# DRAM-to-DRAM additions of the halves of w_down: 128 rows outermost, in quarters of 32 rows

## The chip, the cores and the metric

The kernel runs on one core of a Trainium2 chip. The metric is the device time of one execution in microseconds (us). TensorE (PE) multiplies matrices, VectorE (DVE), ScalarE (ACT) and GpSimd (POOL) do elementwise work, SyncE (SP) only issues transfers. Transfers are issued from SP (and a few from ACT) on one kind of queue and from POOL on another, and all of them run on the core's 16 DMA engines.

## The reference

One layer of a bidirectional mixer is followed by a convolutional feed-forward network, over 1024 latent tokens and 128 prompt tokens of width 1024. The part that matters here is the feed-forward network (FFN_HIDDEN is 2816):

```python
def conv_ffn(h, w_up, conv_w, conv_b, w_down, grid):
    u = dw_conv(h @ w_up, conv_w, conv_b, grid)
    gate, up = jnp.split(u, 2, axis=-1)
    return (jax.nn.silu(gate) * up) @ w_down
```

The result is scaled, added to the residual and normalised. Everything is float32; the kernel splits each operand of a product into a high and a low part and multiplies three times (high by high, high by low, low by high).

## The kernel before

**Both products of the network use seven block products instead of eight** (the Strassen-Winograd scheme), so sums of blocks of the weights are needed. For `w_up` the sums are made in SBUF by POOL, for `w_down` they are made in DRAM, by transfers.

**The up stage** runs over 22 channel blocks, `for c in range(NHID + 1)`; block c is 128 gate and 128 up columns. For each block PE does the seven products `up(c, p)` (line 1322), two halves of the prompt's product (`up_prompt`, line 1526) and two transposes. ACT copies the prompt's result once a block (`late`, line 1615; one such instruction for each block, which makes it a good clock of the stage). DVE does the 3x3 convolution (line 1462) and the prompt's width-3 convolution (line 1479).

POOL works one block ahead: it makes the low parts of the weights (line 62, called from `split_slots`), the sums of `w_up` (`weight_sums`, lines 1313 to 1316), the product of gate and up (line 1558) and sums over tokens (lines 1416 to 1419, every second block). It issues, in its own order, the store of the block's result (`scr_g`, line 1559, 576 KB), the store of the token sums (`scr_s`, line 1420, 1 MB, every second block), and the transfers on `w_down` described below. One such instruction of POOL stands between its elementwise instructions, and what comes later on POOL waits until it is issued.

`load_row` (line 1293) loads the raw weights of a later block into the tile `ra` (and `sr`) from SP: four transfers of 256 KB for each block. `ra` holds one block, so a load is issued only when POOL has read the old contents, and POOL's next `weight_sums` (line 1313) waits until it has landed. PE then waits for the low parts (`wul`, line 62).

**The sums of w_down.** `w_down` is (2816, 1024). With p = 0..127, j = 0..10 and h = 0, 1, row (2j + h) * 128 + p is row p of pair j of half h. Four DRAM scratch tensors `scr_t[i]` of shape (11, 128, 512) are filled: `scr_t[0]` and `scr_t[2]` by copying one block and adding another, `scr_t[1]` and `scr_t[3]` by copying `scr_t[0]` and `scr_t[1]` and adding another block. A copy is one transfer of 2816 KB (line 1430). An addition is a transfer with `accum_op=ALU.add`, which reads its destination and its source and writes the destination; it is issued in four pieces of 3, 3, 3 and 2 values of j (line 1435). That makes 20 transfers, 4 copies and 16 additions, in a list `sums_todo`. `second_half` takes one from the list for each block from the second on, right after the product of gate and up:

```python
        last = nc.gpsimd.tensor_tensor(accg, accg, accu, op=ALU.mult)
        nc.gpsimd.dma_start(scr_g[c], accg)
        if sums_todo and c > 0:
            with tc.issue_after(last.ins):
                sums_todo.pop(0)()
```

So each block of the up stage has one of these transfers, followed in POOL's queue by the store of `scr_g`. The order in the list is: two copies, four pieces of `scr_t[0]`, four of `scr_t[2]`, a copy from `scr_t[0]` to `scr_t[1]`, four pieces, a copy from `scr_t[1]` to `scr_t[3]`, four pieces.

**The down stage** runs seven products of 11 pairs (`product`, line 1732) and the prompt's (line 1783). `load_pair` loads, for each pair j, one block of tokens (`scr_g`, `scr_s`) and one of weights (`w_down`, or `scr_t[i][j]` for the products 4 to 7), on SP's queue, in a fixed sequence that begins before the up stage is over. `load_gates` puts the load of `modrC` in the same queue, and `make_gates` (line 1663) needs it between the last pairs of the first product.

Of the kernel before, what the change touches and what calls it, by code (L numbers as in the profile page):

```python
# [13 lines left out]
ALU = mybir.AluOpType  # L14
# [3 lines left out]
P = 128  # L18
# [7 lines left out]
NPAIR = 11  # L26
# [20 lines left out]
def kernel(ctx: ExitStack, tc: tile.TileContext, ins, outs, stop=None):  # L47
    nc = tc.nc
# [40 lines left out]
    scr_t = [dram.tile([NPAIR, P, 512], F32, name=f"scr_t{i}") for i in range(4)]  # L89
# [72 lines left out]
    w_down = ins["w_ffn_down"][0]  # L162
# [37 lines left out]
    lo_t, hi_t, lo_f, hi_f = slice(0, 512), slice(512, NS), slice(0, 512), slice(512, D)  # L200
# [167 lines left out]
    for i in range(2):  # L368
        nc.vector.memset(modA[i], 0.0)
        t = modA[i][:, :]  # L370
# [1040 lines left out]
    def token_sums(j):  # L1411
# [10 lines left out]


    halves = [
        [w_down.rearrange("(j h p) f -> h j p f", h=2, p=P)[h][:, :, fs] for fs in (lo_f, hi_f)] for h in range(2)
    ]
    sums_todo = []

    def sum_copy(i, src):
        sums_todo.append(lambda: nc.gpsimd.dma_start(scr_t[i], src))  # L1430

    def sum_add(i, src):
        for j in range(0, NPAIR, 3):
            js = slice(j, min(j + 3, NPAIR))
            sums_todo.append(lambda js=js: nc.gpsimd.dma_start(scr_t[i][js], src[js], accum_op=ALU.add))

    sum_copy(0, halves[0][1])
    sum_copy(2, halves[1][1])
    sum_add(0, halves[0][0])
    sum_add(2, halves[0][1])  # L1440
    sum_copy(1, scr_t[0])
    sum_add(1, halves[1][1])
    sum_copy(3, scr_t[1])
    sum_add(3, halves[1][0])

    def conv_rows(u, ch, acc, ra=0, rb=NROW):
# [400 lines left out]
def build(nc, shapes, outs_kind="ExternalOutput", stop=None):  # L1847
    ins = {
        n: nc.dram_tensor(f"in_{n}_dram", s, dt, kind="ExternalInput").ap() for n, (s, dt) in shapes.items()
    }  # L1850
    outs = [
        nc.dram_tensor(f"out_{i}_dram", s, F32, kind="ExternalOutput").ap() for i, (s, _) in enumerate(_OUTS)
    ]
    with tile.TileContext(nc, schedule_with_timeline_sim=True) as tc:
        kernel(tc, ins, outs, stop)
# [14 lines left out]
```

## Time and profile before

| what | value |
|---|---|
| median of 3 runs | 1804.22 us (1801.51 to 1809.65) |
| the profiled execution, its own time | 1807.15 us |
| its span from first to last instruction | 1805.4 us |
| PE busy | 1635.6 us, 91% of the span |
| DVE, ACT, POOL busy | 1189.3, 754.0, 738.9 us |
| mean granted TensorE clock | 0.947 |

In the page's second part the span is cut into 40 slices of 45 us. The up stage fills slices 21 to 34, the down stage the rest. The line PEclk is the clock that TensorE was granted, in tenths of full speed; a matmul takes longer where it is lower. Times "to landing" run from the issue of a transfer to the last of its bytes. In the chain of waits, "DMA" is time in which the next instruction waited for a transfer.

### The profile page before, as it was taken

The page shows a single profiled execution, that of the slowest core. Times are in us where ns is not written, and L with a number is a line of the kernel's source. Part 1 is how long each engine was busy: PE and PEld are TensorE (multiplying, and loading weights), DVE is VectorE, ACT ScalarE, POOL GpSimd, SP SyncE. Part 2 cuts the span into 40 slices and gives each one's busy share as a digit, 9 for nine tenths or more (in the row PEclk, how much of TensorE's full clock was granted, in tenths as well). Part 3 has the DMA queues.
Part 4 walks back from the last instruction along what each step waited for, and adds up shares of the span by engine and source line. Part 5 has one row for each costly group of instructions (what it writes and reads, how often), then busy time and mean ns, then how long its engine had stood idle before and what let it go on. Part 6 is the DMA issues. An engine that isn't in the chain of part 4 may idle for free.

```text
span 1805.4 us, 24012 instructions
## 1 busy us (share of the span) xinstructions
PE 1635.6 (91%) x9050; PEld 1367.4 (76%) x9050; DVE 1189.3 (66%) x1720; ACT 754.0 (42%) x1397; POOL 738.9 (41%) x535
## 2 busy tenths in 40 slices
PE   7999989999999998898789978778787888799998
PEld 2788867998999998786568856656676677578886
DVE  4555453365766768546799967657676787758765
ACT  4433434434544354215554423323333343356544
POOL 2401111232423231112579958667775878400001
PEclk9999997999999999999899998888898899999999
DMA  9133350231413231638213533324433435678863
GB/s 361 53 117 112 105 166 36 78 97 44 129 39 108 66 128 49 251 137 298 93 46 133 162 99 94 99 67 105 145 95 91 137 114 157 200 261 323 304 192 123
DMA packets 191117, 244.37 MB, mean 135 GB/s; under 512 B 38900, under 2 KB 135394, under 8 KB 188954
## 3 DMA queue, kind: packets, MB, share of 16 engines
q1 hardware_dynamic: 142583, 168.54, 29.0%
q0 software_dynamic: 47808, 73.63, 13.1%
q8 instruction: 71, 1.16, 0.3%
q10 hardware_dynamic: 611, 0.68, 0.1%
q14 instruction: 44, 0.36, 0.1%
HBM read 186.95 MB, written 78.71 MB: 147 GB/s over the span
## 4 chain that ended last, share of the span: by engine, by line
PE 59%; DMA 17%; POOL 12%; DVE 6%; issue 4%; ACT 1%; SPq 1%; POOLq 0%; DVEq 0%; ACTq 0%
PE mm L580 15%; DMA ra<-in_w_ffn_up_dram 12%; PE mm L594 6%; POOL wul L62 5%; PE u L1322 5%; PE lv L862 5%; PE xb L1732 5%; PE yb L1732 5%; PE mm L720 3%; PE yb L1783 2%; PE u L1215 2%; DMA scr_g<-acc 2%; PE o L938 1%; PE x L903 1%; PE mm L485 1%
## 5 line engine op out<-in xcount | busy, mean ns | idle before, releaser
L1462 DVE SCALAR_TENSOR_TENSOR acc<-u,convc,acc 128x945 f32<-128x945 f32 (+2 forms) x352 | 426.8, 1218 | 12.1 <-ACT acc L1450 5.7
L62 POOL TENSOR_TENSOR wl<-raw,wh 128x1024 fp32r<-128x1024 f32 x42 | 102.5, 2444 | 272.5 <-ACT wh L123 255.2
L580 PE MATMUL mm<-h1h,wh 128*128 128x384 f32 x528 | 184.2, 349 | 0.1
L580 PE MATMUL mm<-h1l,wh 128*128 128x384 f32 x528 | 180.6, 342 | 0.0
L580 PE MATMUL mm<-h1h,wl 128*128 128x384 f32 x528 | 180.6, 342 | 0.0
L62 POOL TENSOR_TENSOR wul<-sr,wuh 128x512 fp32r<-128x512 f32 (+1 forms) x68 | 134.4, 1978 | 11.4 <-ACT wuh L1308 11.1
L862 PE MATMUL lv<-Q,m 64*128 64x128 f32 (+1 forms) x1008 | 126.2, 295 | 12.5 <-DVE Q L871 6.7
L879 DVE COPY_PREDICATED S<-masks,lv 128x384 f32<-128x384 uint8 x168 | 98.8, 588 | 57.6 <-PE lv L862 57.5
L62 POOL TENSOR_TENSOR wul<-ra,wuh 128x1024 fp32r<-128x1024 f32 x46 | 128.3, 2788 | 13.3 <-ACT wuh L123 7.2
L855 ACT ACTIVATE m<-k 128x384 f32<-128x384 f32 x126 | 69.8, 556 | 140.3 <-DVE k L873 118.1
L862 PEld LDWEIGHTS lv<-Q,m 64*128 64x128 f32 (+1 forms) x1008 | 107.3, 191 | 26.7 <-issue 11.0
L871 DVE TENSOR_TENSOR Q<-Q,fb 128x384 f32<-128x384 f32 x126 | 90.3, 717 | 56.0 <-PE lv L862 55.6
L1322 PE MATMUL u<-b22h,wul 128*128 128x512 f32 x88 | 47.3, 537 | 65.8 <-POOL wul L62 65.8
L580 PEld LDWEIGHTS mm<-h1h,wh 128*128 128x128 f32 x528 | 99.8, 189 | 5.5 <-issue 3.7
L1707 POOL TENSOR_TENSOR sq<-sq,mhalf 128x1 f32<-128x1 f32 x9 | 11.1, 1237 | 222.5 <-DVE sq L1704 222.5
L1479 DVE SCALAR_TENSOR_TENSOR acc<-x,convc,acc 128x127 f32<-128x127 f32 x88 | 30.3, 344 | 108.2 <-ACT acc L1475 108.2
L580 PEld LDWEIGHTS mm<-h1l,wh 128*128 128x128 f32 x528 | 99.8, 189 | 1.5 <-issue 0.8
L580 PEld LDWEIGHTS mm<-h1h,wl 128*128 128x128 f32 x528 | 99.7, 189 | 0.7 <-issue 0.6
L1308 ACT ACTIVATE wuh<-ra 128x1024 fp32r<-128x1024 f32 x44 | 46.3, 1051 | 100.6 <-DMA ra<-in_w_ffn_up_dram 87.4
L123 ACT ACTIVATE wh<-raw 128x1024 fp32r<-128x1024 f32 x55 | 58.1, 1058 | 67.6 <-DMA raw<-in_w_in_dram 23.3
L1313 POOL TENSOR_TENSOR sr<-ra 128x512 f32<-128x512 f32 x22 | 30.8, 1402 | 132.4 <-DMA ra<-in_w_ffn_up_dram 129.8
L594 PE MATMUL mm<-wh,h1h 128*128 128x256 f32 x288 | 83.2, 289 | 0.0
(344 smaller groups left out, 4747.8 us busy)
## 6 DMA issues: line engine op xcount, KB each, us to landing
ra<-in_w_ffn_up_dram SPq DMA_DIRECT2D x88, 256.0 KB, 10.3
raw<-in_w_in_dram SPq DMA_DIRECT2D x32, 512.0 KB, 4.4
raw<-in_w_ada_dram SPq DMA_DIRECT2D x32, 512.0 KB, 3.7
scr_g<-acc POOLq DMA_DIRECT2D x22, 576.0 KB, 24.9
scr_s<-late POOLq DMA_DIRECT2D x11, 1024.0 KB, 16.0
scr_t<-in_w_ffn_down_dram POOLq DMA_DIRECT2D x12, 768.0 KB, 27.3
wa<-in_w_ada_dram SPq DMA_DIRECT2D x16, 512.0 KB, 5.9
raw<-in_w_out_dram SPq DMA_DIRECT2D x13, 512.0 KB, 10.0
```

What stands on the lines that cost most here:

```text
L62: return eng.tensor_tensor(out, full, hi.bitcast(F32), op=ALU.subtract)
L123: nc.scalar.activation(hi, raw, AF.Copy)
L580: mm(ps, a[:, kt, :], h[kt][b], start=(n == 0), stop=(n == 23))
L594: mm(ps, h[kt][t // 3][:, ts_], a[:, kt % 4, :], start=(n == 0), stop=(n == 23))
L720: mm(ps, lhs, ws[f][wi][:, cs], start=(f + n == 0), stop=(f == 6 and n == 2))
L855: nc.scalar.activation(aps(kmix, 0, [[2 * h, NB], [h, 2], [1, h]]), aps(kf_, 0, [[2 * h, NB], [BL + h, 2], [1, h]]), AF.Copy)
L862: last = mm(ps[:, i, :], kmix[r0:r1, i * P : (i + 1) * P], aps(Qf_, i * P, dims, r0, r1), start=True, stop=True,)
L871: nc.vector.tensor_tensor(qm, qm, aps(ff_, 2 * h - 1, [[BL - h, 2], [2 * h, NB], [0, h]]), op=ALU.mult)
L879: nc.vector.copy_predicated(S_, masks[:, lev : lev + 1, :].to_broadcast([P, 3, P]), ps)
L1322: last = mm(dst, W[x][:, a, kt, :], HB[y][b][:, kt, :], start=(start and n == 0), stop=(stop and n == 11), skip_group_check=True,)
L1462: last = nc.vector.scalar_tensor_tensor(o, u3[:, r0 + dy : r1 + dy, c0 + dx : c1 + dx], wc(3 * (dy + 1) + dx + 1), o, op0=ALU.mult, op1=AL ...
L1732: anchor["down"] = mm(banks[i], w[a][:, ts_], w[b][:, 512:1024], start=(start and j == 0 and n == 0), stop=(j == NPAIR - 1 and n == 2), sk ...
```

## The change

The two sides of every copy and addition get another order of dimensions: row p outermost, then pair j. The sources become (128, 11, 512) views of `w_down`, and `sums` are (128, 11, 512) views of the same scratch tensors. An addition is again four pieces, but a piece is now 32 of the 128 rows of all 11 pairs (704 KB) instead of all 128 rows of 3 or 2 pairs (768 or 512 KB). The bytes of each scratch tensor, the list of 20 transfers and its order stay.

In the built program the number and order of instructions on PE, DVE, ACT and SP are the same as before, with the same number of transfers. On POOL the sizes of the 20 transfers differ, and in one of the 22 blocks the store of `scr_s` stands behind one elementwise instruction instead of ahead of it. Before, a copy's destination was written as 1408 rows of 512 and its source as 11 x 128 x 512; an addition's as 384 (or 256) rows and 3 (or 2) x 128 x 512; a copy from `scr_t` to `scr_t` was 64 pieces of 11264 values on both sides. After, all of them are 128 x 11 x 512 or 32 x 11 x 512 on both sides.

```diff
     halves = [
-        [w_down.rearrange("(j h p) f -> h j p f", h=2, p=P)[h][:, :, fs] for fs in (lo_f, hi_f)] for h in range(2)
+        [w_down.rearrange("(j h p) f -> h p j f", h=2, p=P)[h][:, :, fs] for fs in (lo_f, hi_f)] for h in range(2)
     ]
+    sums = [t.rearrange("j p f -> p j f") for t in scr_t]
     sums_todo = []
 
     def sum_copy(i, src):
-        sums_todo.append(lambda: nc.gpsimd.dma_start(scr_t[i], src))
+        sums_todo.append(lambda: nc.gpsimd.dma_start(sums[i], src))
 
     def sum_add(i, src):
-        for j in range(0, NPAIR, 3):
-            js = slice(j, min(j + 3, NPAIR))
-            sums_todo.append(lambda js=js: nc.gpsimd.dma_start(scr_t[i][js], src[js], accum_op=ALU.add))
+        for q in range(0, P, 32):
+            qs = slice(q, q + 32)
+            sums_todo.append(lambda qs=qs: nc.gpsimd.dma_start(sums[i][qs], src[qs], accum_op=ALU.add))
 
     sum_copy(0, halves[0][1])
     sum_copy(2, halves[1][1])
     sum_add(0, halves[0][0])
     sum_add(2, halves[0][1])
-    sum_copy(1, scr_t[0])
+    sum_copy(1, sums[0])
     sum_add(1, halves[1][1])
-    sum_copy(3, scr_t[1])
+    sum_copy(3, sums[1])
     sum_add(3, halves[1][0])
```

## The prediction

> **What bounds the kernel now.** I read the page first: the share of each engine, the slices, and the chain that ended last.
>
> ```profile
> span 1805.4 us, 24012 instructions
> ...
> PE   7999989999999998898789978778787888799998
> ...
> PEclk9999997999999999999899998888898899999999
> ...
> PE 59%; DMA 17%; POOL 12%; DVE 6%; issue 4%; ACT 1%; SPq 1%; POOLq 0%; DVEq 0%; ACTq 0%
> PE mm L580 15%; DMA ra<-in_w_ffn_up_dram 12%; PE mm L594 6%; POOL wul L62 5%; PE u L1322 5%; PE lv L862 5%; PE xb L1732 5%; PE yb L1732 5%; PE mm L720 3%; PE yb L1783 2%; PE u L1215 2%; DMA scr_g<-acc 2%; PE o L938 1%; PE x L903 1%; PE mm L485 1%
> ```
>
> PE carries the chain, except that 12% of it, over 200 us, is a load of up weights into `ra`, and that PE falls to 7 and 8 tenths, with a lower clock, in the slices of the up stage. So I went to that stage. The one ACT instruction for each channel block (line 1615) is its clock; these are its rows for the blocks up to the first addition and from there to the last block, and behind them engine busy time for a pair of blocks with copies, a pair with additions, and the whole stretch with additions:
>
> ```profile
> L1615 ACT ACTIVATE late<-x x4: 385/386/386, 944.7 to 1012.7; 128x256 f32<-128x256 f32 x4
> L1615 ACT ACTIVATE late<-x x18: 384/385/386, 1012.7 to 1528.9; 128x256 f32<-128x256 f32 x18
> core 0: us, PE busy (x) PEld busy (x) DVE busy (x) ACT busy (x) POOL busy (x), PEclk, DMA share, GB/s
> 967.40:1012.70 45.30, 45.30 (x221) 37.33 (x220) 43.65 (x47) 20.93 (x28) 43.54 (x30) 1.00 0.61 215
> 1129.40:1194.30 64.90, 52.26 (x221) 41.71 (x220) 43.72 (x47) 21.14 (x29) 44.92 (x30) 0.84 0.35 89
> 1012.70:1528.90 516.20, 429.04 (x1872) 344.42 (x1870) 371.51 (x392) 179.76 (x238) 375.59 (x245) 0.89 0.40 108
> ```
>
> Until 1012.7 a block takes (1012.7 - 944.7) / 3 = 22.67 us, PE is busy all of it and the clock is full: PE bounds. From there 17 blocks take 516.2 / 17 = 30.4 us. The same 221 matmuls take 52.26 us instead of 45.30 (the clock is 0.84), and the rest of the 64.90 PE idles. The excess is 516.2 - 17 x 22.67 = **130.8 us**: 516.2 - 429.0 = 87 of idle PE, the rest a lowered clock after the idle time. Whom PE waits for, and one block's chain:
>
> ```profile
> PE u L1322 <- POOL wul L62: 65.8, 13, 8.0
> PE u L1322 <- DVE acc L1462: 21.4, 7, 5.5
> POOL sr L1313 <- DMA ra<-in_w_ffn_up_dram: 129.4, 14, 11.6
> 1151.01 1.92 POOL scr_t L1435
> ...
> 1154.63 1.34 POOL scr_g L1559
> ...
> 1160.86 0.37 SPq L1293
> ...
> 1161.28 16.57 DMA ra<-in_w_ffn_up_dram
> ...
> 1178.01 0.75 POOL sr L1313
> ```
>
> PE waits for POOL's low parts, POOL for the load, and the load takes 16.6 us from its issue to the end of the wait. It is issued 9.9 us after the block's addition (1151.01 to 1160.86). Times to landing in microseconds say what delays it: the additions of 3 pairs and of 2, the copies, then loads and stores with no such transfer about, beside a copy, and beside an addition:
>
> ```profile
> scr_t<-in_w_ffn_down_dram POOLq DMA_DIRECT2D x12, 768.0 KB, 27.3
> scr_t<-in_w_ffn_down_dram POOLq DMA_DIRECT2D x4, 512.0 KB, 27.1
> scr_t<-in_w_ffn_down_dram POOLq DMA_DIRECT2D x2, 2816.0 KB, 14.6
> scr_t<-scr_t POOLq DMA_DIRECT2D x2, 2816.0 KB, 10.9
> ra<-in_w_ffn_up_dram SPq DMA_DIRECT2D x6, 256.0 KB, 3.0
> scr_g<-acc POOLq DMA_DIRECT2D x1, 576.0 KB, 3.1
> ra<-in_w_ffn_up_dram SPq DMA_DIRECT2D x4, 256.0 KB, 8.9
> scr_g<-acc POOLq DMA_DIRECT2D x1, 576.0 KB, 12.7
> ra<-in_w_ffn_up_dram SPq DMA_DIRECT2D x4, 256.0 KB, 10.3
> scr_g<-acc POOLq DMA_DIRECT2D x1, 576.0 KB, 25.3
> ```
>
> 768 KB take as long as 512 KB: an addition's time doesn't go with its bytes. What the two kinds share is 128 rows in each pair. So I read it as one lane for each pair: 27.3 / 128 = 0.213 us a row of 2 KB, in 3 or 2 lanes at once, while 11 pairs without an addition take half of it. A load of `ra` lies across all engines and ends with its slowest; a few engines that alternate between addition and load make it 10.3 instead of 3.0, and loads that follow each other there add up to 16.6. The store of `scr_g`, queued behind the addition, lands in 25.3 instead of 3.1.
>
> **The change part by part.** *The additions.* A piece is now 32 x 11 = 352 rows with the 32 outermost. If the outermost index is what is spread, 16 engines get 352 / 16 = 22 rows each, 22 x 0.213 = 4.7 us. Below: the copy inside DRAM reads and writes 5632 KB in 10.9 us, and a piece moves 3 x 704 = 2112 KB, 4.1 us at that rate. Above: no more than the 11 lanes that the copy shows, 32 x 0.213 = 6.8 us. I take 4.7, the row's own price. All three end before the loads are issued (9.9 us later), so the addition is gone when they start and they should land in the 3.0 us of an undisturbed one. What if this cover fails is the third rival.
>
> No row shows an outermost 32. The Trainium skill ("DMA: Bandwidth & Descriptors", section "Why a DMA increments its semaphore by 16 and not by 1") says that a transfer uses the largest number of engines up to 16 that divides the outermost sizes of both sides: that gives 3, 2 and 11 before, as the landings above bear out, and 16 after.
>
> *The copies.* They go from 11 lanes (14.6 us), or 64 long pieces (10.9 us), to 1408 rows on as many engines as can be had: 88 rows for each of 16 at 14.6 / 128 = 0.114 us make 10.0 us. Gain or loss is nothing: a block with the 14.6 us copy beside it, loads at 8.9, already runs at 22.67. Were that cover gone, a block would pay at most the 7.7 us (130.8 / 17) that an addition costs it now.
>
> *POOL's issue of them.* Its duration in ns (min/median/max), for additions, copies from `w_down` and copies of `scr_t`:
>
> ```profile
> L1435 POOL DMA_DIRECT2D scr_t<-in_w_ffn_down_dram x16: 1902/1942/2678, 1021.7 to 1534.0; - x16
> L1430 POOL DMA_DIRECT2D scr_t<-in_w_ffn_down_dram x2: 1134/1134/1134, 973.8 to 997.7; - x2
> L1430 POOL DMA_DIRECT2D scr_t<-scr_t x2: 554/554/555, 1282.5 to 1434.6; - x2
> ```
>
> 384 rows and 256 rows cost the same 1.9 us and 1408 rows 1.1, so the price seems to follow the rows of one lane, not all rows: 128 with an addition 1.94, 22 after, hence between 0.55 and 1.94, and I take about 0.8. POOL's pair of blocks then needs 44.92 - 2 x 1.1 = 42.7 us, less than PE's 45.3 and less than the 43.54 of the pair with copies that ran at PE's pace. So PE sets the pace and all **130.8 us** go. The order on every engine but POOL is unchanged, nothing new is queued behind a wait, and DVE's 43.7 a pair stays below 45.3.
>
> *The change of stages.* The last additions also delay the first product of the down stage:
>
> ```profile
> SPq L120 <- DMA scr_g<-acc: 19.0, 1, 19.0
> PE yb L1663 <- DMA modrC<-scr_modC: 5.8, 1, 5.8
> PE xb L1732 <- DVE acc L1479: 4.5, 1, 4.5
> PE xb L1732 <- POOL wl L62: 1.7, 1, 1.7
> ACT acc L1475 <- DMA scr_g<-acc: 4.7, 1, 4.7
> 1537.45 29.02 DMA scr_g<-acc
> 1550.00:1600.00 50.00, 42.88 (x172) 32.88 (x173) 27.60 (x21) 20.60 (x24) 10.83 (x7) 0.93 0.73 263
> ```
>
> The store issued at 1537.45 lands 29 us later, behind the last addition; SP's queue stands 19.0 us for it, and the load of `modrC` behind it makes PE wait 5.8. With the store landing near 3.1 us, SP goes on some 20 us earlier and this wait goes, and the 1.7 for a late split of a loaded pair with it: 7.5 us. The 4.5 may partly go (ACT, ahead of that DVE instruction, waits 4.7 us for another such store), and so may 7% of 42.88 = 3.0 us of lowered clock; I leave both in place. Between nothing and 5.8 + 4.5 + 1.7 + 3.0 = 15.0, I take 7.5.
>
> *The sum.* Against the span: 1805.4 - 130.8 - 7.5 = 1667.1. The profiled execution took 1807.15, 2.9 above the median of 1804.22; from the median, 1804.2 - 138.3 = **1666 us**, 7.7% faster.
>
> **The rivals.** *POOL becomes the bound.* If its issue stays at 1.94 us, a pair needs 44.92, and with the idle time that it keeps in the pair with copies (45.30 - 43.54 = 1.76) a block takes 23.34: 0.67 x 17 = 11 us given back, 1677. With the dearest issue seen (2.68) it is 24.08 a block, 24 us, 1690. For it: POOL and PE lie within 0.4 us a pair. Against it: the price of 1.94 seems to follow the rows of a lane.
>
> *It doesn't spread.* If 32 outermost rows still go to two or three engines, an addition stays at 27 us or more and all is as before, 1804. Against it: the landings by pairs above, and the 3.1 us of a 576 KB store of 128 rows.
>
> *Slow rows.* Now successive rows of a piece are 1 MB apart in `w_down` and 256 KB in `scr_t`, where they were 4 KB and 2 KB apart, and no row shows what that costs. Up to 9.9 / 22 = 0.45 us a row (2.1 times as much) nothing happens. At 27.3 / 22 = 1.24 us (5.8 times) an addition holds all engines as long as it now holds three, and the 130.8 come back; halfway it is about 1731.
>
> The Trainium skill's row on HBM row pitch at large powers of two (same page, section "Latency and other measured facts") speaks for this: 207 GB/s at a pitch of 512 KiB, 164 at 2 MiB and 103 at 4 MiB against 214 without. Were it to hold here, an estimate from that page is a factor of 1.03 to 1.3, at most 2.1, so 4.9 to 9.9 us for a piece, just inside the cover.
>
> *Slower than before.* The same mechanism, past its deciding point of 5.8: then the four copies too hold all engines, 88 rows x 0.114 x 5.8 = 58 us each instead of 10.9 to 14.6, in blocks that now run at PE's pace. Four blocks pay 7.7 us more, with nothing gained: 1804 + 31 = 1835. Against it: a factor of nearly 6 on plain rows of 2 KB.
>
> **How the numbers follow.** Forecast 0.69; POOL 0.18; slow rows, between, 0.07; no spreading 0.03; slower 0.03. The first case's own range is 1804.2 - 130.8 - 15.0 - 2.7 (the fastest run lies 2.7 below the median) = 1655 to 1674 (no gain at the change of stages). POOL's case extends it to 1690; 0.13 is left outside. About 0.5% is what a measurement of this kernel can tell from no change: faster 0.94, same 0.03, slower 0.03.
>
> **What would show it.** Right: additions landing in 4 to 7 us, `scr_g` in under 8, loads of `ra` near 3, the load gone from the chain, 22.7 us between the instructions of line 1615, clock 1.0 through the stage, POOL's issue below 1 us, no wait for `modrC`. Wrong: additions above 10 us with loads beside them (slow rows), about 27 (no spreading), or blocks of 23 to 24 us with PE waiting for line 62 while loads land early (POOL).

## The result, and the profile after

The changed kernel took 1666.54 us (median of 4 runs, 1666.05 to 1673.29), the kernel before 1802.87 us beside it (4 runs, 1801.18 to 1809.65). The ratio is 0.9246, with a 95% interval of 0.9212 to 0.928: 7.5% faster. The prediction was 1666 us.

These are lines of the changed kernel's page: span, PE's busy tenths and clock in 40 slices, and the chain that ended last by engine and by line.

```profile
span 1664.3 us, 24010 instructions
...
PE   7999998999999999889996999999999998999997
...
PEclk9999997999999999999997999999999999999999
...
PE 86%; DVE 6%; DMA 4%; issue 1%; POOL 1%; ACT 1%; SPq 0%; POOLq 0%; DVEq 0%; ACTq 0%
PE u L1322 24%; PE mm L580 16%; PE xb L1733 7%; PE mm L594 6%; PE lv L862 6%; PE yb L1733 5%; PE x L1527 4%; PE mm L720 3%; PE yb L1784 2%; PE u L1215 2%; PE o L938 1%; PE x L903 1%; PE mm L485 1%; PE o L940 1%; PE ada L1007 1%
```

The load of `ra`, 12% of the chain before, is gone from it. What takes its place is the up stage's matmul itself: line 1322 rises from 5% to 24%, and PE's slices there are nines where they were sevens and eights. (Lines from 1427 on have moved by one.)

Where the time went is read by cutting both spans at the first and the last ACT instruction of line 1615 (1616 after). The rows are: before the up stage's blocks, the 21 intervals between them, and the rest; first of the kernel before, then of the changed one. Columns are length, busy time of PE, PEld, DVE, ACT, POOL, then clock, DMA share and GB/s.

```profile
0.00:917.20 917.20, 858.00 (x5651) 740.89 (x5651) 539.00 (x1028) 395.81 (x936) 241.80 (x217) 0.97 0.37 122
917.20:1528.90 611.70, 522.11 (x2310) 420.69 (x2310) 464.09 (x486) 223.01 (x296) 460.47 (x297) 0.90 0.40 111
1528.90:1805.40 276.50, 255.47 (x1090) 205.84 (x1090) 186.19 (x208) 135.17 (x166) 36.63 (x23) 0.97 0.68 233
```

```profile
0.00:915.10 915.10, 858.49 (x5651) 741.76 (x5651) 541.17 (x1028) 395.81 (x936) 241.32 (x217) 0.97 0.37 122
915.10:1396.10 481.00, 478.38 (x2310) 393.53 (x2310) 464.02 (x486) 221.47 (x296) 451.75 (x297) 1.00 0.50 142
1396.10:1664.30 268.20, 253.28 (x1090) 205.21 (x1090) 188.84 (x208) 134.78 (x166) 35.25 (x23) 0.99 0.70 239
```

Of the 141.1 us between the spans, 611.7 - 481.0 = 130.7 come from the up stage, 276.5 - 268.2 = 8.3 from what follows, and 2.1 from what stands ahead of it, where nothing was edited. In the up stage the same 2310 matmuls take 478.4 us instead of 522.1, because the clock is 1.00 instead of 0.90, and PE idles 2.6 us instead of 89.6.

Times to landing of the changed kernel, from its page and its list of transfers (KB each, then the median in us):

```profile
ra<-in_w_ffn_up_dram SPq DMA_DIRECT2D x88, 256.0 KB, 3.0
scr_g<-acc POOLq DMA_DIRECT2D x22, 576.0 KB, 5.2
scr_t<-in_w_ffn_down_dram POOLq DMA_DIRECT2D x16, 704.0 KB, 7.1
scr_t<-in_w_ffn_down_dram POOLq DMA_DIRECT2D x2, 2816.0 KB, 12.3
scr_t<-scr_t POOLq DMA_DIRECT2D x2, 2816.0 KB, 12.2
```

An addition lands in 7.1 us instead of 27.3, the store behind it in 5.2 instead of 24.9, and a load of `ra` in the 3.0 of an undisturbed one instead of 10.3.

### The profile page after: what moved, and what is told of

The parts are those of the page before. It is cut to its first block, busy times and chain, and to the rows that moved or that the text cites. A ratio compares the mean times of both kernels' runs of the same rounds, so it can differ in the third digit from the quotient of the medians.

```text
span 1664.3 us, 24010 instructions
## 1 busy us (share of the span) xinstructions
PE 1590.2 (96%) x9050; PEld 1340.5 (81%) x9050; DVE 1194.0 (72%) x1720; ACT 752.1 (45%) x1397; POOL 728.3 (44%) x535
## 2 busy tenths in 40 slices
DMA packets 164621, 244.15 MB, mean 147 GB/s; under 512 B 11124, under 2 KB 107618, under 8 KB 162586
## 3 DMA queue, kind: packets, MB, share of 16 engines
q0 software_dynamic: 21312, 73.41, 14.2%
## 4 chain that ended last, share of the span: by engine, by line
PE 86%; DVE 6%; DMA 4%; issue 1%; POOL 1%; ACT 1%; SPq 0%; POOLq 0%; DVEq 0%; ACTq 0%
PE u L1322 24%; PE mm L580 16%; PE xb L1733 7%; PE mm L594 6%; PE lv L862 6%; PE yb L1733 5%; PE x L1527 4%; PE mm L720 3%; PE yb L1784 2%; PE u L1215 2%; PE o L938 1%; PE x L903 1%; PE mm L485 1%; PE o L940 1%; PE ada L1007 1%
## 5 line engine op out<-in xcount | busy, mean ns | idle before, releaser
L62 POOL TENSOR_TENSOR wul<-sr,wuh 128x512 fp32r<-128x512 f32 (+1 forms) x68 | 123.2, 1814 | 25.9 <-ACT wuh L1308 25.7
L62 POOL TENSOR_TENSOR wul<-ra,wuh 128x1024 fp32r<-128x1024 f32 x46 | 118.8, 2583 | 9.2 <-ACT wuh L1308 6.0
L873 DVE TENSOR_TENSOR k<-k,fb 128x384 f32<-128x384 f32 x126 | 76.2, 608 | 6.9 <-ACT m L855 2.9
L594 PE MATMUL mm<-wl,h1h 128*128 128x256 f32 x288 | 81.0, 281 | 0.0
L594 PE MATMUL mm<-wh,h1l 128*128 128x256 f32 x288 | 80.9, 281 | 0.0
```

The lines of the kernel that those rows point to most:

```text
L62: return eng.tensor_tensor(out, full, hi.bitcast(F32), op=ALU.subtract)
L594: mm(ps, h[kt][t // 3][:, ts_], a[:, kt % 4, :], start=(n == 0), stop=(n == 23))
L873: nc.vector.tensor_tensor(km, km, aps(ff_, BL + 2 * h - 1, [[-(BL + h), 2], [2 * h, NB], [0, h]]), op=ALU.mult)
```

## The experiments

What is common to all: from profile to profile the part ahead of the first block varies by more than 10 us (the first block's ACT instruction stood at 912 to 926 us in the profiles below, where the programs do the same). So the up stage is read from its own clock, the time from the first to the last of the 22 instructions, 481.0 us in the changed kernel, and the part behind it by itself, 268.2 us.

### The copies or the additions

One kernel has the new copies and the old additions, the other the old copies and the new additions.

```diff
     def sum_add(i, src):
-        for q in range(0, P, 32):
-            qs = slice(q, q + 32)
-            sums_todo.append(lambda qs=qs: nc.gpsimd.dma_start(sums[i][qs], src[qs], accum_op=ALU.add))
+        src = src.rearrange("p j f -> j p f")
+        for j in range(0, NPAIR, 3):
+            js = slice(j, min(j + 3, NPAIR))
+            sums_todo.append(lambda js=js: nc.gpsimd.dma_start(scr_t[i][js], src[js], accum_op=ALU.add))
```

> New copies, but the 16 additions as before (3, 3, 3 and 2 pairs outermost, 128 rows each). Theory (what counts is over how many DMA engines an addition's rows are spread, since that sets how long it stands beside the loads of ra): additions land near 27 us, blocks with one take 30 us as before, 1800 us (1795 to 1808). Rival (the copies matter too, by their share of the 18 transfers that became short): 4 of 20 transfers, so some 25 us of the 138 won, 1775.

```diff
     def sum_copy(i, src):
-        sums_todo.append(lambda: nc.gpsimd.dma_start(sums[i], src))
+        sums_todo.append(
+            lambda: nc.gpsimd.dma_start(*(t.rearrange("p j f -> j p f") for t in (sums[i], src)))
+        )
```

> Old copies (11 pairs outermost, or 64 long pieces), new additions. Theory: the copies cost nothing in either form, 1666 us (1662 to 1672), additions landing near 7 us. Rival (copies matter): 1690.

Measured: 1802.87 us with the old additions and 1664.3 us with the old copies, beside 1801.51 us for the kernel before. The ACT instruction of line 1615, in each kernel's own numbering, first of the old additions, then of the old copies:

```profile
L1617 ACT ACTIVATE late<-x x22: 362/385/386, 913.0 to 1523.3; 128x256 f32<-128x256 f32 x22
```

```profile
L1618 ACT ACTIVATE late<-x x22: 362/385/386, 913.1 to 1394.1; 128x256 f32<-128x256 f32 x22
```

The up stage takes 610.3 us with the old additions and 481.0 with the old copies. The old additions land in 27.3 and 27.0 us again, the new ones beside the old copies in 7.2. The additions are the whole of the gain in the up stage; the copies are worth nothing in either form. The rival with 25 us for the copies falls.

### The same bytes, fewer lanes

These two keep additions in four pieces of about the same bytes and change the outermost size, and with it the order of the rows. The first has the changed kernel's pieces with the 11 pairs outermost:

```diff
-            sums_todo.append(lambda qs=qs: nc.gpsimd.dma_start(sums[i][qs], src[qs], accum_op=ALU.add))
+            sums_todo.append(lambda qs=qs: nc.gpsimd.dma_start(
+                *(t[qs].rearrange("p j f -> j p f") for t in (sums[i], src)), accum_op=ALU.add
+            ))
```

> The changed kernel's pieces (32 rows of 11 pairs, the same bytes), with the 11 pairs outermost instead of the 32 rows, so neighbouring rows of a pair follow each other. Theory: 11 lanes of 32 rows, 32 x 0.215 us + some 2 us = 9 us to landing against 7 in the changed kernel; it ends just before the loads are issued, so 1666 to 1672 us. Rival (what helped is the new composition or the new order of rows, not the number of lanes): landing as in the changed kernel, 7 us, if composition; 27 us and 1800 if the order of the rows.

```diff
-        for q in range(0, P, 32):
-            qs = slice(q, q + 32)
-            sums_todo.append(lambda qs=qs: nc.gpsimd.dma_start(sums[i][qs], src[qs], accum_op=ALU.add))
+        for js in (slice(0, 6), slice(6, NPAIR)):
+            for qs in (slice(0, 64), slice(64, P)):
+                sums_todo.append(
+                    lambda js=js, qs=qs: nc.gpsimd.dma_start(
+                        *(t[qs, js].rearrange("p j f -> j p f") for t in (sums[i], src)), accum_op=ALU.add
+                    )
+                )
```

> Four pieces of 64 rows of 6 or 5 pairs with the pairs outermost. Both theories: 6 or 5 lanes of 64 rows, 64 x 0.215 + 2 = 16 us to landing. Theory A (a price begins when the addition outlasts the 9.9 us until the loads, and grows in proportion up to the 8.2 us that an addition of 27.3 us costs): 6 / 17.4 x 8.2 = 2.8 us for each of 16 additions, 1711 us. Theory B (a price begins only when a load's wait exceeds the some 8 us of POOL's own work behind its issue): loads at 6 to 9 us, no price, 1666 to 1675 us.

The additions' landing, with 11 pairs outermost, and then with 6 and with 5:

```profile
scr_t<-in_w_ffn_down_dram POOLq DMA_DIRECT2D x16, 704.0 KB, 9.1
```

```profile
scr_t<-in_w_ffn_down_dram POOLq DMA_DIRECT2D x8, 768.0 KB, 14.7
...
scr_t<-in_w_ffn_down_dram POOLq DMA_DIRECT2D x8, 640.0 KB, 14.8
```

Eleven lanes of 32 rows land in 9.1 us, as expected, and cost nothing (1667.82 us, up stage 480.9); neither rival holds, the composition with its 7 us or the order of the rows with its 27. In the second kernel 768 KB and 640 KB land alike, as 768 and 512 KB did before: it is the 64 rows of a lane that count. The kernel took 1691.99 us, and its up stage 495.2 us (922.3 to 1417.5), 14.2 more than the changed kernel's, or 0.9 for each addition. That is neither theory A's 45 us nor theory B's nothing. What POOL waits for in its up stage from 1017 us on (us in total, times, longest) shows why:

```profile
L1620 ACT ACTIVATE late<-x x22: 360/384/386, 922.3 to 1417.5; 128x256 f32<-128x256 f32 x22
POOL sr L1313 <- DMA ra<-in_w_ffn_up_dram: 18.9, 9, 3.7
```

Nine loads came late, by 3.7 us at most. In the trace six intervals are longer, every second one, with 23.3 to 27.1 us, while those between stay at 22.7. Theory B's mechanism fits, a load's wait against POOL's own work, but its 8 us of work hold for half of the blocks only. Behind the issue of the loads POOL has 8.0 us of work in one kind of block and about 6.1 in the other, where it has to wait some 3.3 us more, until 9.4 us after that issue.

### One addition for each sum, halves, and none

```diff
-        for q in range(0, P, 32):
-            qs = slice(q, q + 32)
+        for q in range(0, P, 64):
+            qs = slice(q, q + 64)
```

> Additions in 2 pieces of 64 rows instead of 4 of 32: 8 additions, the last in block 12 instead of 20, none left at the change of stages. Theory (spread over 16 engines, and a price only when a load waits longer than POOL works behind its issue): 44 rows a lane, 44 x 0.215 + 2.3 = 11.8 us to landing, loads of ra near 5, blocks stay at 22.67, and at the change of stages the two waits of 1.6 and 1.7 us for a pair loaded beside the last addition go: 1663 us, 3 less than the changed kernel. Rival (a price begins when the addition outlasts the 9.9 us before the loads): 8 x 0.9 = 7 us more, 1670.

```diff
-        for q in range(0, P, 32):
-            qs = slice(q, q + 32)
-            sums_todo.append(lambda qs=qs: nc.gpsimd.dma_start(sums[i][qs], src[qs], accum_op=ALU.add))
+        sums_todo.append(lambda: nc.gpsimd.dma_start(sums[i], src, accum_op=ALU.add))
```

> Each sum is one addition of all 128 rows of 11 pairs, rows outermost: 4 additions instead of 16, on 16 lanes of 88 rows, 3 + 88 x 0.19 = 20 us to landing (the line through 7.1 us at 22 rows and 27.3 at 128). Theory (what counts is how long an addition stands beside the loads, on however many engines): an addition of 20 us costs its block between the 1.8 us of e4's every-other 14.7 us and the 8.2 of 27.3, some 5 us: 1666 + 4 x 5 = 1686, less 3 at the change of stages, 1683; loads of ra beside it at 8 to 10 us. Rival (16 lanes share the burden, so a load loses little on each): blocks at 22.67, loads below 6, 1663.

```diff
         for q in range(0, P, 32):
-            qs = slice(q, q + 32)
-            sums_todo.append(lambda qs=qs: nc.gpsimd.dma_start(sums[i][qs], src[qs], accum_op=ALU.add))
+            sums_todo.append(lambda: None)
```

> The 16 additions are left out (scr_t then holds single blocks of w_down instead of sums); the 4 copies stay. Theory (16 additions spread over 16 engines cost the up stage nothing, and some 3 us at the change of stages): 1663 us, as with halves, blocks of 22.67. Rival (they still cost by their share of the DMA engines): 1640 to 1655.

> The changed kernel once more, unedited, as the measure for the three beside it: 1666 us (1663 to 1670), blocks of 22.67 us.

Measured beside each other, as a ratio to the kernel before: the changed kernel again 0.9228 (0.9189 to 0.9267, median 1670.63 us), halves 0.9221 (0.9187 to 0.9256, 1667.8 us), no additions 0.921 (0.9176 to 0.9244, 1665.94 us). Their up stages take 481.0, 481.1 and 481.1 us. The first and the last block of each, in this order:

```profile
L1616 ACT ACTIVATE late<-x x22: 360/385/386, 921.8 to 1402.8; 128x256 f32<-128x256 f32 x22
L1616 ACT ACTIVATE late<-x x22: 360/384/386, 912.0 to 1393.1; 128x256 f32<-128x256 f32 x22
L1615 ACT ACTIVATE late<-x x22: 362/385/386, 923.3 to 1404.4; 128x256 f32<-128x256 f32 x22
```

So the changed kernel's 16 additions cost the up stage nothing that can be seen, and the rival of 1640 to 1655 us without them falls. A half lands in 12.0 us and so outlasts the 8.2 to 9.5 us that lie between it and the loads in this kernel, and it costs nothing either: the rival of halves at 7 us falls. Its loads do come late at times (POOL's waits, as above), but POOL's idle time takes it up:

```profile
POOL sr L1313 <- DMA ra<-in_w_ffn_up_dram: 4.3, 5, 1.8
```

Behind the up stage the three take 269.4, 266.7 and 266.0 us, and the first profile of the changed kernel 268.2. The 3 us expected of halves are not shown: a wait of 1.4 to 1.6 us goes and one of 1.7 shrinks to 1.0, but one of 1.1 us for `modrC` and one of 0.8 for its gate come, so PE's waits for the first products fall from 5.7 to 5.5 us only (3.4 without additions). The intervals of the whole times overlap too.

The single additions of all rows (16 lanes of 88 rows) took 1702.46 us. Their landing (the group of 6 holds the 2 copies too), and the clock of the stage:

```profile
scr_t<-in_w_ffn_down_dram POOLq DMA_DIRECT2D x6, 2816.0 KB, 20.2
```

```profile
L1614 ACT ACTIVATE late<-x x22: 362/385/386, 926.4 to 1434.3; 128x256 f32<-128x256 f32 x22
```

The up stage takes 507.9 us, 26.9 more, on average 6.7 for each of four additions where 5 were expected; the rest of the 1702 is a late start (926 us). In the trace the loads beside these additions land in 10.4 to 11.4 us, as late as beside the old three lanes. The rival that 16 lanes share the burden falls: here how long an addition stands beside the loads decides, and not on how many engines it stands.

### Two rows more

```diff
-        for q in range(0, P, 32):
-            qs = slice(q, q + 32)
+        for a, b in ((0, 34), (34, 68), (68, 98), (98, P)):
+            qs = slice(a, b)
```

> The changed kernel's rows-outermost pieces, of 34, 34, 30 and 30 rows instead of 32 each. Theory (the number of lanes is the largest number up to 16 that divides the outermost size): 34 rows on 2 lanes of 187 rows, 3 + 187 x 0.19 = 39 us to landing; 30 rows on 15 lanes of 22, 7 us. The eight additions of 34 rows outlast a block and cost 8.2 us and more each: 1666 + 8 x 8.2 to 8 x 14 = 1730 to 1780. Rival (rows outermost are dealt out one by one over 16 engines): 34 rows make 33 rows on the fullest lane, 9 us, and 1666 to 1670.

From its list of transfers, and the clock of the stage:

```profile
scr_t<-in_w_ffn_down_dram POOLq DMA_DIRECT2D x8, 748.0 KB, 39.6
...
scr_t<-in_w_ffn_down_dram POOLq DMA_DIRECT2D x8, 660.0 KB, 7.8
...
L1616 ACT ACTIVATE late<-x x22: 361/385/386, 915.8 to 1491.9; 128x256 f32<-128x256 f32 x22
```

34 rows outermost land in 39.6 us, 30 in 7.8. The kernel took 1761.91 us; its up stage 576.1 us (915.8 to 1491.9), 95.1 more, 11.9 for each of the eight long additions. So it is not the order of dimensions as such that wins: two rows more give 95 of the 130.7 us back. They come back by another way in part: these additions outlast their block, and the `scr_g` store behind them lands some 37 us after its issue. In the chain of waits from 1010 to 1491 us that store has 22.8% and the load of `ra` 11.2%, and ACT waits for the store 46.8 us in four waits. The Trainium skill ("DMA: Bandwidth & Descriptors", section "Why a DMA increments its semaphore by 16 and not by 1") has the rule: the largest number up to 16 that divides the outermost sizes. The trace agrees: 39.6 and 7.8 us are what two lanes of 187 rows and fifteen of 22 give, and the count of small packets at the end of this text fits these numbers of lanes.

### More work for POOL

```diff
         eng.tensor_tensor(r["s3"], r["11"], r["21"], op=ALU.subtract)
+        if c > 1:
+            eng.tensor_tensor(r["s3"][:, 0:3], r["11"][:, 0:3], r["21"][:, 0:3], op=ALU.subtract)
```

> The changed kernel, and POOL makes three quarters of one weight sum a second time in each block (same values), some 0.95 us, about what an addition's issue got cheaper (1.94 to 1.09). Prediction's rival (POOL keeps its idle time of 1.76 us a pair and becomes the bound): a pair needs 43.6 + 1.9 + 1.7 = 47.2 us, 0.95 a block, 20 blocks: 1685. Theory (PE paces and POOL's idle time is slack that shrinks): POOL's 45.5 a pair against PE's 45.3, 0.1 a block: 1667 to 1670.

Measured: 1672.88 us, ratio 0.9248 (0.9213 to 0.9282). The ACT instruction of each block, and engine busy time in a pair of blocks (columns as above):

```profile
L1618 ACT ACTIVATE late<-x x22: 360/385/387, 915.0 to 1405.4; 128x256 f32<-128x256 f32 x22
```

```profile
1101.70:1148.30 46.60, 45.52 (x221) 37.39 (x220) 44.20 (x47) 20.88 (x28) 45.12 (x32) 1.00 0.51 130
```

The whole time can't be told from the changed kernel's (the intervals overlap), but the up stage can: 490.4 us, 9.4 more, 0.5 for each of the 20 added instructions. That lies between the rival's 19 us and the theory's 2. POOL is busy 45.12 us of this pair, and the pair takes 46.60 instead of 45.3: POOL does begin to bound. Over the last 17 blocks it is busy 382.3 us of 394.9, where the changed kernel has 366.8 of 385.5: of 15.5 us more work 9.4 lengthen the stage, and 6.1 come out of idle time. Some of POOL's other instructions also stand in another order in this program, so the share that the added ones alone would cost is not shown.

## Why the prediction was right

**The bound and its cause.** Right. The additions, through the loads of `ra` that they delayed, held the stage back. Only additions count, the load is gone from the chain, and POOL no longer waits for it. The delay was predicted to fall away in full; 130.7 of 130.8 us did, the lowered clock with it. The `scr_g` store was delayed too (24.9 us), but the kernel before hardly waited for it: from 900 to 1500 us its chain of waits has 35.4% for the load of `ra` and no such store, and ACT waits for the store 4.9 us in seven waits. Only with 34 rows does the store carry much of the chain. No run delays the one without the other.

**One lane for each outermost index.** Right for outermost sizes of 3, 5, 6 and 11. Of larger ones the largest divisor up to 16 counts, as the rule cited in the prediction has it: 16, 2 and 15 lanes for 32, 34 and 30 rows. The size was off: 22 rows at 0.213 us were to land in 4.7 us, at most 6.8; they took 7.1. The step that failed is to take the row's price as 27.3 / 128, with nothing fixed. A line through 7.1 us at 22 rows and 27.3 at 128 has 0.19 us a row and 3 us fixed; it gives 9.0, 15.1, 19.7 and 38.5 us at 32, 64, 88 and 187 rows, where 9.1, 14.7, 20.2 and 39.6 were measured (12.0 at 44 rows is 0.7 above it). The 7.1 us still end before the loads, so the missing 2.4 us cost nothing; they lie just outside the prediction's own sign of 4 to 7.

**The copies.** Nothing gained or lost, right, though they landed in 12.3 and 12.2 us instead of 10.0.

**POOL's issue.** The price rises with the rows of a lane, right in the main, but it came out at 1.1 us instead of 0.8, above the sign of "below 1 us". The row of the 16 additions (ns, min/median/max), and busy time in a pair of blocks, both of the changed kernel:

```profile
L1436 POOL DMA_DIRECT2D scr_t<-in_w_ffn_down_dram x16: 1024/1092/1162, 1017.1 to 1401.2; - x16
```

```profile
1056.00:1101.30 45.30, 45.30 (x221) 37.29 (x220) 43.69 (x48) 20.92 (x28) 43.55 (x30) 1.00 0.50 128
```

A pair of blocks needs 43.55 us of POOL instead of the 42.7 worked out, beside PE's 45.30, which is busy throughout. The rival that POOL becomes the bound was close: an engine that is 1.75 us from it in a pair has no room for the 0.95 us a block that the last experiment was to add. The rival kept POOL's idle time fixed; the 6.1 us that came out of it there show a part of it to be slack, and the 19 us worked out in that way were twice the 9.4 measured.

**The cover.** The prediction had a price begin when an addition outlasts the 9.9 us before the loads. The 9.9 us are those of one kind of block: before, the loads follow 9.8 to 10.0 us behind an addition or 8.7 to 8.8, by turns, and with the shorter issue of the changed kernel 9.1 or 8.0. And outlasting it isn't where the price begins: 12.0 us cost nothing, 14.7 cost 0.9 us an addition, 20.2 cost 6.7. Neither had any effect here. A load that meets the end of an addition is late by little (4.8 to 7.1 us instead of 3.0 beside the halves), and POOL's work and idle time covered that.

**The change of stages.** 8.3 us instead of 7.5, from other parts than named. What PE still waits for there, from 1390 to 1450 us of the changed kernel:

```profile
PE xb L1733 <- DVE acc L1480: 2.6, 1, 2.6
PE xb L1733 <- POOL wl L62: 1.7, 1, 1.7
PE xb L1733 <- ACT wh L123: 1.6, 1, 1.6
```

The 5.8 us for `modrC` went, as said. The 1.7 us for a late split, which was to go, stayed, and 1.6 us came beside it; the 4.5 us for DVE fell to 2.6, and 255.47 - 253.28 = 2.2 us came from shorter busy time of PE, whose clock rose from 0.97 to 0.99. The step that failed is the late split: the prediction put its 1.7 us down to SP's wait for the store. With that wait gone they stayed, behind a load of `w_down` that took 9.4 us beside the last addition, and only the run without additions is free of them.

**Slow rows.** Not seen, beyond a few per cent. Rows 1 MB apart (22, 44, 88 and 187 a lane) and rows 4 KB apart (32, 64 and 128) lie within 0.7 us in 12 and 1.1 us in 40 of the line above. The Trainium skill's row on power-of-two pitches ("DMA: Bandwidth & Descriptors", section "Latency and other measured facts"), from which the prediction estimated factors of 1.03 to 2.1, does not show here in its larger factors; its figures are for rows of 16 KiB, not 2 KB, and a factor of 1.03 would be too small to tell.

**The number.** That the median came within 0.6 us of 1666 is in part luck: the up stage's term is exact, but the 8.3 us at the change of stages came from other parts than the 7.5, and the first block of the changed kernel alone stood at 915.1 us in one profile and at 921.8 in another.

## What to carry to other kernels

The time to landing of these transfers was first a question of how many engines their outermost sizes could be dealt to; compare two transfers of different bytes and the same landing to find it, and choose an outermost size that 16 divides. A transfer that nobody waits for is not free: its cost is that of the loads and stores that it delays, and here that cost began where the delay exceeded the work that the waiting engine had in hand. After such a change look at the engine next in line, here POOL with 43.55 us in a pair of 45.30.

## What was not expected of the hardware

The number of packets. The two pages count all transfers of an execution, first before, then after:

```profile
DMA packets 191117, 244.37 MB, mean 135 GB/s; under 512 B 38900, under 2 KB 135394, under 8 KB 188954
```

```profile
DMA packets 164621, 244.15 MB, mean 147 GB/s; under 512 B 11124, under 2 KB 107618, under 8 KB 162586
```

38900 - 11124 = 27776 packets under 512 B are gone, though no small transfer was removed. In the trace of before they are packets of 8 bytes beside the additions and the old copies. Their number is that of the engines a POOL transfer left out, each with as many packets as a used one: 12 additions x 13 engines x 128, 4 x 14 x 128, and 2 copies x 5 engines x 64 make 27776. The other runs bear it out, by their pages' counts above the 11124: 2560 with 11 pairs outermost (16 x 5 x 32), 10753 with 6 and 5 (8 x 10 x 64 and 8 x 11 x 64 make 10752), and 21120 with 34 and 30 rows (8 x 14 x 187 and 8 x 1 x 22). That is a second sign of the number of lanes, beside the landings. That issuing from POOL costs for these packets too is not shown, but it would fit a price by the rows of a lane: an addition's issue took 1.1 us with 22 rows a lane, 1.4 with 44 and 64, 1.9 with 128 and 3.3 with the 187 of 34 rows outermost. It isn't a line, though: 88 rows on 16 lanes took 2.0, more than 128 on three.
